# A two-block transformer layer on one core: every SBUF tile given whole 128-byte lines

## The chip, the core and the metric

The kernel runs on one core of one Trainium2 chip. The metric is the device time of one execution in microseconds (us), as the median of several runs. A core has a tensor engine (TensorE), which multiplies matrices into PSUM; a vector engine (VectorE) and a scalar engine (ScalarE), which work elementwise; GpSimd; and SyncE (SP), which here only issues DMAs. [...] The change concerns where in SBUF a tile begins.

## The reference, cut to what matters

Two blocks on 256 tokens of 1024 features, everything in float32. The first is modulated by a condition `c`:

```python
mod = silu(c) @ w_ada + b_ada                       # nine vectors of 1024
h = x + 0.5 * g1 * swiglu(modulate(rmsnorm(x)), w_ff1_gate, w_ff1_up, w_ff1_down)
h = h + g2 * token_mixing(modulate(rmsnorm(h)))     # gated linear attention and block attention
h = h + 0.5 * g3 * swiglu(modulate(rmsnorm(h)), w_ff2_gate, w_ff2_up, w_ff2_down)
x = rmsnorm(h)
x = x + hybrid_mixer(rmsnorm(x))                    # gated delta rule and mLSTM
x = x + memory_cross_attention(rmsnorm(x), rmsnorm(mem))
x = x + peer_ffn(rmsnorm(x))                        # 16384 experts, 8 heads, the 16 best of each
return rmsnorm(x)
```

`peer_ffn` scores every token against 2 × 128 keys per head, picks 16 experts per head, and sums gate × gelu(u_e · x) × v_e over them. The kernel forms the products with both whole tables (16384 × 1024 each) and uses the gates as a mask.

## The kernel before, in words

**Products.** Nearly all time goes into products of weights with 256 tokens. To keep float32 accuracy, each operand is split into a high and a low part of type float32r (hi = rounded copy, lo = rest), and three products are summed: hi·hi, hi·lo, lo·hi. A weight chunk of 128 x 1024 values (512 KB) is loaded by an SP DMA into a tile `raw` (L253), ScalarE casts it to `whi` (L254), VectorE subtracts to get `wlo` (L255). `raw` has three buffers and `whi`, `wlo` two, in each of two pools (`wa`, `wb`), taken in turn, so up to six chunks are loaded ahead. In the last part of the program, where only `wa` is left, a third pair of buffers, `wpair`, sits where `hT` was.

There are two forms of product. `linear_steps` has the weights stationary and the activations moving, 256 columns at a time (L305 to L307):

```python
mm(ps, wh, xh[:, kk, :], start=(kk == 0), stop=False)
mm(ps, wh, xl[:, kk, :], start=False, stop=False)
mm(ps, wl, xh[:, kk, :], start=False, stop=(kk == KT - 1))
```

`tm_steps` and `v_mm` have the activations stationary and the weights moving, 512 columns at a time. Every matmul has the line L192, that of the helper `mm(o, l, r)`, where `l` is the stationary operand and `r` the moving one. The profile names them as out<-moving,stationary: `mm<-uh,whi` has `uh` moving. `uh`, `ul` are the split activations (one pair of tiles for all norms), `hh`, `hl` the split hidden tile of an FFN (one pair in each), `mh`, `ml` the split memory, `oah` to `obl` and `xoh`, `xol` the split results of attentions, `wh`, `wl` a split column of expert weights. The products of attention and recurrences are plain float32 (`sm` tiles).

**Stages** in order of time (us of the profiled execution): modulation and first norm (0 to 38), FFN1 gate and up (38 to 172), FFN1 down and memory values (172 to 240), mixer 1 (240 to 435), FFN2 (435 to 636), memory keys and values, mixer 2 (to 860), cross attention (to 915), expert queries, first expert table with the choice of experts (to 1145) and with the gate matrices (to 1395), second expert table (to the end).

**Order of the work.** The program is written as generators that are woven together; a scheduler of the framework then orders each engine's instructions by priority and dependencies. A load into a tile has to wait for whoever last used that memory, so the place of a tile in SBUF also decides what its load waits for and when it is put into SP's queue.

**Tiles and their places.** A tile comes from a pool, `pool.tile(shape, dtype, name=..., tag=..., bufs=...)`; its size in a partition is rounded up to a multiple of 32 bytes, and tiles follow each other. Since `epsc` and `mean` have one column, `cols` 220 and so on, the large tiles behind them begin at any multiple of 32 bytes. The built program has these places, by the remainder of the byte address by 128:

| tiles | before | with the change |
|---|---|---|
| `uh`, `ul`, `hT`, `raw`, `whi`, `wlo`, `wpair` | 64 | 0 |
| `hh`, `hl` of FFN1 | 0 | 0 |
| `hh`, `hl` of FFN2 | 96 | 0 |
| `mh`, `ml`, `oah` to `obl`, `xoh`, `xol` | 96 | 0 |
| `wh`, `wl` | 64 | 0 |
| float32: `dm`, `m`, `dt`, `xs` | 0 | 0 |
| float32: `cvgq`, `cvgk` and the like | 64 | 0 |
| float32: `gv`, `at`, `gq`, `gk`, `xV`, `xpt` | 96 | 0 |

Slices that a product reads within a tile are whole multiples of 512 bytes, so they have their tile's remainder.

Of the kernel before, what the change touches and what calls it, by code (L numbers as in the profile page):

```python
# [33 lines left out]
# column pack: name -> number of columns  # L34
# [109 lines left out]
def _consts():  # L144
    """Arrays that depend on shapes alone."""
# [12 lines left out]
    # bucket of each distance; index x stands for distance 255 - x  # L158
# [15 lines left out]
    # selectors of packed rows: 0-3 row h; 4-7 rows h, 32+h, 64+h; 8-11 minus row 32+h  # L174
# [10 lines left out]
# ----------------------------------------------------------------- device code  # L185
def body(tc, A, out):
# [7 lines left out]
    cp = es.enter_context(tc.tile_pool(name="cp", bufs=1))  # L194
    wa = es.enter_context(tc.tile_pool(name="wa", bufs=2))
    pmm = es.enter_context(tc.tile_pool(name="pmm", bufs=4, space=PSUM))
    psm = es.enter_context(tc.tile_pool(name="psm", bufs=4, space=PSUM))
    dr = es.enter_context(tc.tile_pool(name="dr", bufs=1, space=DRAM))


    # ---- constants and small inputs
# [25 lines left out]
    # ---- weights: raw chunk -> exact pair (hi, lo), 12 bits each  # L227
    class Weights:
# [6 lines left out]
        def ahead(self, src, shape):  # L235
            """make the next chunk now, for a product further on"""
# [23 lines left out]
    def split(hi, lo, src):  # L260
        """src (SBUF or PSUM, fp32) -> hi, lo (float32r)"""
# [8 lines left out]
    def later(n=100000):  # L270
        """instructions that fill what the following ones leave idle"""
# [5 lines left out]
    def weave(main, side, n, m):  # L277
        """n steps of main, then m of side, in turn"""
# [9 lines left out]
    def linear_steps(w, KT, ms, xh, xl, evac):  # L288
        """feature-major output tiles [128, 256]; w [MT, 128, KT, 128]"""
# [26 lines left out]
    def tm_steps(w, n, xh, xl, evac):  # L316
        """token-major output [128 tokens, 512]; w [n, 4, 128, 2, 512]"""
# [17 lines left out]
    def sum_sq(pool, src, w=None):  # L335
        """mean over the 1024 features of (src * w)^2, a column per 128 tokens (PSUM)"""
# [11 lines left out]
    def rsqrt(pool, ms):  # L348
        """1 / sqrt(ms + eps), columns"""
        r = pool.tile([P, 2], F32, name="rr", tag="rr", bufs=4)  # L350
        act.activation(r, ms, AF.Sqrt, bias=epsc)  # L351
        r2 = pool.tile([P, 2], F32, name="rr2", tag="rr2", bufs=4)
# [3 lines left out]
    def spread(pool, r):  # L356
        """columns [tokens, 2] -> the row of 256 tokens on every partition (PSUM)"""
# [18 lines left out]
    def norm_apply(pool, src, r, hi, lo, a, b):  # L376
        """hi + lo = src * r * a + b"""
# [11 lines left out]
    # ================================================================ block 1  # L389
    wb_es = ExitStack()  # L390
    wb = wb_es.enter_context(tc.tile_pool(name="wb", bufs=2))
    W.pools.append(wb)
    npool = wb_es.enter_context(tc.tile_pool(name="npool", bufs=1))
    b1_es = ExitStack()
    kvp = b1_es.enter_context(tc.tile_pool(name="kvp", bufs=1))
# [5 lines left out]
    # silu(c) on every partition; mod = w_ada^T silu(c) + b_ada, feature-major  # L401
    kt_es = ExitStack()
    kt = kt_es.enter_context(tc.tile_pool(name="kvt", bufs=1))
# [8 lines left out]
    def ada_steps(js, cb=cb, bufs=None):  # L412
        """columns js of the modulation; bufs: memory for the weights"""
        o = _COFF["bada"][0]
        for j in js:
# [6 lines left out]
            if j // 8 in (1, 4, 7):  # L422
                # norm * (1 + scale)
# [13 lines left out]
    # K^T and V of the memory, kept in DRAM until the cross attention; made in pieces  # L437
    # where the tensor engine would wait for a norm
# [41 lines left out]
    # the modulation of the first norm, shift and scale in turn  # L480
# [14 lines left out]
    def ffn(name, i, fill, more):  # L495
        with tc.tile_pool(name=name, bufs=1) as fp:
# [43 lines left out]
    # ---------------------------------------------------------------- mixer 1  # L540
    with tc.tile_pool(name="mx", bufs=1) as mp:
        # bias[p, k] at distance 128 + p - k, kept at x = 127 - p + k
# [50 lines left out]
        # gate of the normalised GLA output: silu(gog) * norm  # L593
# [4 lines left out]
        # ---- GLA: log decay, cumulated within each 128 tokens  # L598
# [15 lines left out]
        # ---- attention matrices A^T[j, i], merged from levels of halved blocks;  # L614
        # heads of even and odd number sit in different halves of the partitions
# [37 lines left out]
        # between the two 128-token tiles  # L653
# [11 lines left out]
        # ---- outputs, norm per head, gate  # L665
# [4 lines left out]
        oa = [mp.tile([P, 4, P], F32, name="oa", tag="z", bufs=3) for _ in range(2)]  # L670
        for t in range(2):
# [6 lines left out]
            ss = mp.tile([P, 4], F32, name="gss", tag="gss", bufs=2)  # L678
# [9 lines left out]
        def to_fm(src, hi, lo, n):  # L688
            """token-major blocks src(t, h) [128, 128] -> hi, lo [128, n, 256]"""
# [8 lines left out]
        # ---- MoBA: one block of keys, so causal softmax attention  # L698
        def softmax_rows(pool, lg, n, tagp):
            """lg [128, n] -> normalised in place"""  # L700
            mx = pool.tile([P, 1], F32, name="smx", tag=tagp + "mx", bufs=3)
            dve.tensor_reduce(mx, lg, AX.X, OP.max, negate=True)
            sm = pool.tile([P, 1], F32, name="ssm", tag=tagp + "sm", bufs=3)
            act.activation(lg, lg, AF.Exp, bias=mx, accum_out=sm)
            rc = pool.tile([P, 1], F32, name="src", tag=tagp + "rc", bufs=3)
# [23 lines left out]
        # ---- merge; the gates are (1 + tanh(x/2)) / 2, their half is taken at the end  # L729
        g5 = mp.tile([P, 8], F32, name="g5")  # L730
        dve.tensor_scalar(g5, mod[:, 40:48], 0.5, None, OP.mult)
# [20 lines left out]
    # two norms in a row: x = h r1 g, and the mean square of x is r1^2 mean (h g)^2  # L752
# [16 lines left out]
    # ================================================================ block 2  # L769
    with tc.tile_pool(name="hx", bufs=1) as hp:  # L770
# [25 lines left out]
        def conv(ps, name, j, dst):  # L796
            """depthwise causal convolution over the tokens (half of it), then silu(x) =
            (1 + tanh(x/2)) x/2"""
# [51 lines left out]
        # ---- gates: rows 0-3 g_a, 32-35 g_b, 64-67 m_i, 96-99 m_f  # L850
# [534 lines left out]
```

## Time and profile before

| | |
|---|---|
| median of 3 runs | 1763.02 us (1762.89 to 1763.87) |
| profiled execution, its span | 1756.4 us |
| TensorE busy | 1700.8 us, 97% |
| VectorE busy | 1253.9 us, 71% |
| ScalarE busy | 1025.0 us, 58% |
| DMA, mean | 191 GB/s, 336.32 MB |

The profiled execution is known by its span, from its first to its last instruction; the times of the runs are taken around the execution and are some 6.6 us longer. Busy times of TensorE come from modelled ends of pipelined matmuls: a matmul's 0.28 us is the time from its start to its result, and several overlap. What a matmul costs in a row of them is the distance between their starts. TensorE's granted clock is nearly always that of full speed.

### The profile page before, as it was taken

Reading aid. Unit: us, or ns where it says so; the run is one execution under the profiler, and the core shown is the slowest. Engines: PE = TensorE matmul, PEld = TensorE weight load, DVE = VectorE, ACT = ScalarE, POOL = GpSimd, SP = SyncE. Lnnn points to the kernel's source line nnn. Section 1 sums busy time; section 2 is a strip of 40 time slices with the busy share of each in tenths; the row PEclk is TensorE's granted clock in tenths of the full one; section 3 lists DMA queues with packets and bytes.
Section 4 is the critical chain, followed back from the end, with each engine's and each line's share of the span. In section 5 each row is a group of like instructions: output and inputs, shape, how many; then the busy total and the mean of one; then the engine's idle time right before and its main releaser. Section 6 shows DMA issues by size and latency. Waiting matters only on the chain.

```text
span 1756.4 us, 31700 instructions
## 1 busy us (share of the span) xinstructions
PE 1700.8 (97%) x12298; PEld 1603.0 (91%) x12298; DVE 1253.9 (71%) x2223; ACT 1025.0 (58%) x1977; POOL 4.0 (0%) x36
## 2 busy tenths in 40 slices
PE   3999999899999999999989999999999999999998
PEld 2999998899999999888889999999999988888886
DVE  7888677767855569866566689488999755555555
ACT  5556466565644458666654445588877544444544
POOL 0000000000000000000000000000000000000000
PEclk9999999999999999999999999999999999999999
DMA  9888788345855657216325555544444555555554
GB/s 345 326 294 314 222 283 319 121 144 181 287 192 175 186 181 246 91 37 220 131 79 196 177 174 179 192 144 136 142 142 136 192 190 194 192 180 192 192 193 143
DMA packets 97716, 336.32 MB, mean 191 GB/s; under 512 B 10988, under 2 KB 16541, under 8 KB 96926
## 3 DMA queue, kind: packets, MB, share of 16 engines
q1 hardware_dynamic: 94828, 330.63, 55.8%
q10 hardware_dynamic: 2738, 3.68, 0.6%
q8 instruction: 96, 1.57, 0.4%
q14 instruction: 54, 0.44, 0.1%
HBM read 329.02 MB, written 5.25 MB: 190 GB/s over the span
## 4 chain that ended last, share of the span: by engine, by line
PE 90%; DVE 4%; ACT 3%; DMA 2%; issue 2%; SPq 0%; DVEq 0%; ACTq 0%
PE mm L192 81%; PE sm L192 8%; DMA wr<-in_w_ada 1%; DVE wlo L255 1%; DMA mT<-in_memT 0%; ACT whi L254 0%; DVE wr L419 0%; DVE at L651 0%; DVE ac L806 0%; DVE sqa L342 0%; PE sm L693 0%; PE sm L1117 0%; DVE xn L487 0%; PE sm L720 0%; ACT L351 0%
## 5 line engine op out<-in xcount | busy, mean ns | idle before, releaser
L255 DVE TENSOR_TENSOR wlo<-raw,whi 128x1024 fp32r<-128x1024 f32 (+1 forms) x448 | 542.6, 1213 | 255.0 <-ACT whi L254 253.9
L254 ACT CAST whi<-raw 128x1024 fp32r<-128x1024 f32 (+1 forms) x448 | 465.7, 1041 | 402.0 <-PE mm L192 285.6
L192 PE MATMUL mm<-uh,whi 128*128 128x256 f32 x2064 | 592.2, 289 | 9.8 <-ACT whi L254 7.4
L192 PE MATMUL mm<-ul,whi 128*128 128x256 f32 x2064 | 587.7, 286 | 2.5 <-DVE ul L263 2.0
L192 PE MATMUL mm<-uh,wlo 128*128 128x256 f32 x2064 | 586.8, 285 | 0.7 <-DVE wlo L255 0.7
L192 PEld LDWEIGHTS mm<-uh,whi 128*128 128x128 f32 x2064 | 397.4, 193 | 12.0 <-ACT whi L254 8.2
L192 PEld LDWEIGHTS mm<-ul,whi 128*128 128x128 f32 x2064 | 398.0, 193 | 3.7 <-DVE ul L263 2.2
L192 PEld LDWEIGHTS mm<-uh,wlo 128*128 128x128 f32 x2064 | 397.8, 193 | 1.9 <-DVE wlo L255 1.3
L255 DVE TENSOR_TENSOR wpair<-raw,wpair 128x1024 fp32r<-128x1024 f32 x90 | 110.0, 1222 | 82.4 <-ACT wpair L254 82.4
L192 PE MATMUL mm<-uh,wpair 128*128 128x256 f32 x768 | 148.1, 286 | 0.0
L192 PE MATMUL mm<-whi,wh 128*128 128x512 f32 x344 | 133.8, 390 | 1.7 <-ACT wh L262 1.7
L192 PE MATMUL mm<-whi,wl 128*128 128x512 f32 x344 | 134.8, 392 | 0.1
L192 PE MATMUL mm<-wlo,wh 128*128 128x512 f32 x344 | 134.6, 391 | 0.0
L254 ACT CAST wpair<-raw 128x1024 fp32r<-128x1024 f32 x90 | 94.6, 1051 | 65.2 <-PE mm L192 65.2
L192 PEld LDWEIGHTS mm<-uh,wpair 128*128 128x128 f32 x768 | 122.9, 191 | 0.0
L192 PE MATMUL mm<-wpair,wh 128*128 128x512 f32 x336 | 110.2, 389 | 0.0
L192 PE MATMUL mm<-ul,wpair 128*128 128x256 f32 x384 | 108.6, 283 | 0.0
L419 DVE SCALAR_TENSOR_TENSOR wr<-wr,cb 128x1024 f32<-128x1024 f32 x72 | 87.4, 1220 | 19.7 <-DMA wr<-in_w_ada 19.5
L192 PE MATMUL mm<-hh,whi 128*128 128x256 f32 x352 | 98.7, 280 | 0.0
L192 PE MATMUL mm<-hl,whi 128*128 128x256 f32 x352 | 98.6, 280 | 0.0
L192 PE MATMUL mm<-hh,wlo 128*128 128x256 f32 x352 | 98.6, 280 | 0.0
L192 PEld LDWEIGHTS mm<-whi,wh 128*128 128x128 f32 x344 | 64.7, 188 | 15.3 <-ACT wh L262 1.9
(838 smaller groups left out, 2621.9 us busy)
## 6 DMA issues: line engine op xcount, KB each, us to landing
raw<-in_pu SPq DMA_DIRECT2D x128, 512.0 KB, 3.2
raw<-in_pv SPq DMA_DIRECT2D x128, 512.0 KB, 3.2
raw<-in_ff_gu SPq DMA_DIRECT2D x88, 512.0 KB, 4.3
wr<-in_w_ada SPq DMA_DIRECT2D x72, 512.0 KB, 5.9
raw<-in_in_fm SPq DMA_DIRECT2D x34, 512.0 KB, 4.3
raw<-in_ff_dn SPq DMA_DIRECT2D x32, 512.0 KB, 4.1
raw<-in_in_tm SPq DMA_DIRECT2D x24, 512.0 KB, 5.6
raw<-in_in_gab SPq DMA_DIRECT2D x16, 512.0 KB, 4.3
```

The source lines that it names most:

```text
L192: pe.matmul(o, l, r, start=start, stop=stop)
L254: act.copy(hi[:, :n], raw[:, :n])
L255: dve.tensor_tensor(lo[:, :n], raw[:, :n], hi[:, :n].bitcast(F32), OP.subtract)
L419: dve.scalar_tensor_tensor(wr, wr, 1.0, cb, OP.mult, OP.mult, accum_out=mod[:, j:j + 1])
```

## The change

Each pool is wrapped: `Pools` hands out pools, and for those in SBUF a `Lines` object, which makes every tile's size in a partition a multiple of `LINE` = 128 bytes by adding columns at its end, and returns the part that was asked for. To save places, small columns are joined: `rr` and `rr2` of `rsqrt` are two halves of a tile of four columns; the three columns of `softmax_rows` (`smx`, `ssm`, `src`) one tile `sm3`; the two `gss` tiles one; `warm` and the two `fss` tiles one. `g5`, half of eight columns of `mod`, is no tile of its own any more: the scaling is done in `mod` in place. Two tags of `s2` become one. Comments were dropped, so line numbers differ by 35 and more.

```diff
+LINE = 128
+class Pools:
+    def __init__(self, tc):
+        self.tc = tc
+    @contextmanager
+    def __call__(self, **kw):
+        with self.tc.tile_pool(**kw) as pool:
+            yield pool if "space" in kw else Lines(pool)
+class Lines:
+    def __init__(self, pool):
+        self.pool = pool
+    def tile(self, shape, dtype, **kw):
+        n = int(np.prod(shape[1:]))
+        per = LINE // 4
+        if n % per == 0:
+            return self.pool.tile(shape, dtype, **kw)
+        kw.setdefault("tag", kw["name"])
+        t = self.pool.tile([shape[0], -(-n // per) * per], dtype, **kw)[:, :n]
+        if len(shape) == 2:
+            return t
+        d = "abc"[:len(shape) - 1]
+        return t.rearrange(f"p ({' '.join(d)}) -> p {' '.join(d)}", **dict(zip(d, shape[1:])))
...
-    cp = es.enter_context(tc.tile_pool(name="cp", bufs=1))
-    wa = es.enter_context(tc.tile_pool(name="wa", bufs=2))
+    tile_pool = Pools(tc)
+    cp = es.enter_context(tile_pool(name="cp", bufs=1))
+    wa = es.enter_context(tile_pool(name="wa", bufs=2))
...
-        r = pool.tile([P, 2], F32, name="rr", tag="rr", bufs=4)
+        rr = pool.tile([P, 4], F32, name="rr", tag="rr", bufs=4)
+        r, r2 = rr[:, 0:2], rr[:, 2:4]
         act.activation(r, ms, AF.Sqrt, bias=epsc)
-        r2 = pool.tile([P, 2], F32, name="rr2", tag="rr2", bufs=4)
         dve.reciprocal(r2, r)
...
+        gss = mp.tile([P, 2, 4], F32, name="gss")
...
-            ss = mp.tile([P, 4], F32, name="gss", tag="gss", bufs=2)
+            ss = gss[:, t, :]
...
-            mx = pool.tile([P, 1], F32, name="smx", tag=tagp + "mx", bufs=3)
+            c3 = pool.tile([P, 4], F32, name="sm3", tag=tagp + "m3", bufs=3)
+            mx, sm, rc = c3[:, 0:1], c3[:, 1:2], c3[:, 2:3]
...
-        g5 = mp.tile([P, 8], F32, name="g5")
-        dve.tensor_scalar(g5, mod[:, 40:48], 0.5, None, OP.mult)
+        g5 = mod[:, 40:48]
+        dve.tensor_scalar(g5, g5, 0.5, None, OP.mult)
...
+        fss = vp.tile([P, 5], F32, name="fss")
...
-                act.activation(vp.tile([P, 1], F32, name="warm"), epsc, AF.Sqrt)
+                act.activation(fss[:, 4:5], epsc, AF.Sqrt)
...
-            ss = vp.tile([P, 2], F32, name="fss", tag="fss", bufs=2)
+            ss = fss[:, 2 * t:2 * t + 2]
```

All other tiles are written as before; their places move with those in front of them. The counts of instructions of every engine are the same. Their order differs in two places.

SP's queue at the start of FFN2, before (`raw` are weight chunks, `wr` blocks of `w_ada`, `cb` a copy of silu(c)):

```order
L253 DMA raw<-in_w_out 128x1024 x8
L253 DMA raw<-in_xa_k 128x1024 x4
L253 DMA raw<-in_ff_gu 128x1024 x5
L431 DMA cb_5332<-cd 128x1024
L418 DMA wr_5334<-in_w_ada 128x1024
L253 DMA raw<-in_ff_gu 128x1024
L418 DMA wr_5335<-in_w_ada 128x1024
L253 DMA raw<-in_ff_gu 128x1024
L418 DMA wr_5334<-in_w_ada 128x1024
L253 DMA raw<-in_ff_gu 128x1024
```

and with the change:

```order
L288 DMA raw<-in_w_out 128x1024 x8
L288 DMA raw<-in_xa_k 128x1024 x2
L466 DMA cb_5310<-cd 128x1024
L288 DMA raw<-in_xa_k 128x1024 x2
L453 DMA wr_5312<-in_w_ada 128x1024
L288 DMA raw<-in_ff_gu 128x1024
L453 DMA wr_5313<-in_w_ada 128x1024
L288 DMA raw<-in_ff_gu 128x1024
L453 DMA wr_5312<-in_w_ada 128x1024
L288 DMA raw<-in_ff_gu 128x1024
```

The copy `cb` went ahead of two chunks of `xa_k`, and the first blocks of `w_ada` ahead of the chunks of `ff_gu` that had been five in a row. The tiles moved with all others; `cb` lies over the tiles `zb`, `zl` and `oa` of the GLA stage in both, and its load now also waits for TensorE, which read `oa`.

VectorE's queue at the end of FFN1's down product and in the norm of mixer 1, before (`g` is g5, `sqa` the sum of squares of the norm):

```order
L255 TENSOR_TENSOR wlo<-raw,whi 128x1024
L342 TENSOR_TENSOR sqa<-sqa,sq 128x256
L255 TENSOR_TENSOR wlo<-raw,whi 128x1024 x2
L533 SCALAR_TENSOR_TENSOR hT<-mm,half,hT 128x256
L731 TENSOR_SCALAR g_3965<-mod 128x8
L255 TENSOR_TENSOR wlo<-raw,whi 128x1024
L342 TENSOR_TENSOR sqa<-sqa,sq 128x256
L255 TENSOR_TENSOR wlo<-raw,whi 128x1024
```

and with the change, where the scaling now stands with the first columns of that product:

```order
L568 SCALAR_TENSOR_TENSOR hT<-mm,half,hT 128x256
L454 SCALAR_TENSOR_TENSOR wr,mod<-wr,cb 128x1024
L290 TENSOR_TENSOR wlo<-raw,whi 128x1024
L377 TENSOR_TENSOR sqa<-sqa,sq 128x256
L766 TENSOR_SCALAR mod<-mod 128x8
L290 TENSOR_TENSOR wlo<-raw,whi 128x1024
L290 TENSOR_TENSOR wlo<-raw,whi 128x768
L568 SCALAR_TENSOR_TENSOR hT<-mm,half,hT 128x256
```

The scaling, now in `mod` itself, stands some thirty rows earlier; the rows around it are the same.

## Rows read from the trace of the kernel before

**Rows 1.** The page: the span; its section 1, busy time, share of the span and count of instructions of each engine (PE is TensorE, PEld its weight loads, DVE VectorE, ACT ScalarE); the second line of its section 4, the chain of work that ended last, by line.

```profile
span 1756.4 us, 31700 instructions
...
PE 1700.8 (97%) x12298; PEld 1603.0 (91%) x12298; DVE 1253.9 (71%) x2223; ACT 1025.0 (58%) x1977; POOL 4.0 (0%) x36
...
PE mm L192 81%; PE sm L192 8%; DMA wr<-in_w_ada 1%; DVE wlo L255 1%; DMA mT<-in_memT 0%; ACT whi L254 0%; DVE wr L419 0%; DVE at L651 0%; DVE ac L806 0%; DVE sqa L342 0%; PE sm L693 0%; PE sm L1117 0%; DVE xn L487 0%; PE sm L720 0%; ACT L351 0%
```

**Rows 2.** The table of stretches, four of them: start and end in us, length, then for PE, PEld, DVE, ACT and POOL the busy us and the number of instructions, the granted TensorE clock as a share of full speed, the mean busy share of the DMA engines, GB/s moved.

```profile
38.00:172.00 134.00, 133.62 (x1083) 131.94 (x1084) 111.19 (x169) 80.89 (x153) 0.00 (x0) 0.99 0.88 318
440.00:570.00 130.00, 130.00 (x1085) 129.85 (x1084) 85.13 (x121) 69.60 (x115) 0.00 (x0) 1.00 0.67 219
1037.00:1145.00 108.00, 108.00 (x904) 108.00 (x903) 83.34 (x259) 61.56 (x99) 0.00 (x0) 1.00 0.55 181
1145.00:1395.00 250.00, 249.19 (x2116) 248.98 (x2114) 229.93 (x323) 192.00 (x513) 0.00 (x0) 1.00 0.42 141
```

**Rows 3.** The timeline of TensorE in FFN2's up product, two instructions that are eight steps apart, each a matmul of its own in between: start us, us, engine, line, operation, result<-moving operand,stationary operand, array part used, shape of the moving operand.

```profile
499.94 0.28 PE L192 MATMUL mm<-uh,whi 128*128 128x256 f32 x1
...
500.90 0.28 PE L192 MATMUL mm<-uh,wlo 128*128 128x256 f32 x1
```

**Rows 4.** The same in the last stage (experts, second table), two instructions that are twenty steps apart.

```profile
1500.05 0.39 PE L192 MATMUL mm<-whi,wh 128*128 128x512 f32 x1
...
1504.58 0.39 PE L192 MATMUL mm<-wlo,wh 128*128 128x512 f32 x1
```

**Rows 5.** The same in FFN1's down product, nine steps apart.

```profile
199.94 0.28 PE L192 MATMUL mm<-hh,whi 128*128 128x256 f32 x1
...
200.96 0.28 PE L192 MATMUL mm<-hh,whi 128*128 128x256 f32 x1
```

**Rows 6.** The same in FFN2's down product, nine steps apart.

```profile
599.90 0.28 PE L192 MATMUL mm<-hl,whi 128*128 128x256 f32 x1
...
600.96 0.28 PE L192 MATMUL mm<-hl,whi 128*128 128x256 f32 x1
```

**Rows 7.** The same in the product for the values of the memory, six steps apart.

```profile
652.53 0.39 PE L192 MATMUL mm<-whi,ml 128*128 128x512 f32 x1
...
653.93 0.39 PE L192 MATMUL mm<-whi,ml 128*128 128x512 f32 x1
```

**Rows 8.** The timeline of TensorE at three places with plain float32 products, where equal instructions in a row are one line: start of the first, us to the end of the last, operation, operands, shape, count.

```profile
345.83 0.83 PE L192 MATMUL sm<-gv,at 128*128 128x128 f32 x6
...
721.12 0.83 PE L192 MATMUL sm<-cvgq,cvgk 128*128 128x128 f32 x6
...
727.43 0.72 PE L192 MATMUL sm<-dm,m 128*128 128x128 f32 x5
```

**Rows 9.** The groups of TensorE's matmuls with different shapes kept apart: line, operation, operands, shape, count | busy us, mean ns of one (a latency) | idle time before them and what ended it.

```profile
L192 PE MATMUL mm<-uh,whi 128*128 128x256 f32 x2064 | 592.2, 289 | 9.8 <-ACT whi L254 7.4 <-ACT uh L372 1.4 <-ACT uh L262 1.0
...
L192 PE MATMUL mm<-uh,wpair 128*128 128x256 f32 x768 | 148.1, 286 | 0.0
...
L192 PE MATMUL mm<-whi,wh 128*128 128x512 f32 x344 | 133.8, 390 | 1.7 <-ACT wh L262 1.7
L192 PE MATMUL mm<-wpair,wh 128*128 128x512 f32 x336 | 110.2, 389 | 0.0
L192 PE MATMUL mm<-ul,wpair 128*128 128x256 f32 x384 | 108.6, 283 | 0.0
L192 PE MATMUL mm<-hh,whi 128*128 128x256 f32 x352 | 98.7, 280 | 0.0
...
L192 PE MATMUL mm<-wpair,wl 128*128 128x512 f32 x168 | 65.4, 389 | 0.0
L192 PE MATMUL mm<-whi,uh 128*128 128x512 f32 x96 | 37.8, 394 | 0.1
...
L192 PE MATMUL mm<-xoh,whi 128*128 128x256 f32 x64 | 18.0, 287 | 0.0
L192 PE MATMUL mm<-mh,whi 128*128 128x256 f32 x64 | 17.9, 280 | 0.0
...
L192 PE MATMUL mm<-whi,mh 128*128 128x512 f32 x32 | 12.9, 405 | 0.0
...
L192 PE MATMUL mm<-oah,whi 128*128 128x256 f32 x32 | 9.1, 286 | 0.0
```

**Rows 10.** The chain of waits in order of time, three pieces of it: start us, us, what, number of instructions.

```profile
37.99 99.82 PE mm L192 x817
...
152.34 7.47 DMA wr<-in_w_ada
...
1397.19 352.10 PE mm L192 x1561
```

**Rows 11.** The groups of VectorE by line, first from 100 to 172 us (FFN1), then from 470 to 570 us (FFN2): the low half of the FFN's hidden tile.

```profile
L263 DVE TENSOR_TENSOR hl<-sy,hh 128x256 fp32r<-128x256 f32 x12 | 5.0, 419 | 0.0
...
L263 DVE TENSOR_TENSOR hl<-sy,hh 128x256 fp32r<-128x256 f32 x18 | 7.5, 418 | 0.0
```

**Rows 12.** The timeline of the SP queue at the start of FFN2: start us, us, line, what it loads, count.

```profile
421.93 11.80 SPq L253 DMA_DIRECT2D raw<-in_ff_gu  x5
434.59 0.33 SPq L431 DMA_DIRECT2D cb<-cd  x1
434.96 0.42 SPq L418 DMA_DIRECT2D wr<-in_w_ada  x1
```

More of the change, by code (lines that the diff above doesn't have):

```diff
@@ L192, in mm @@
         pe.matmul(o, l, r, start=start, stop=stop)
-    cp = es.enter_context(tc.tile_pool(name="cp", bufs=1))
-    wa = es.enter_context(tc.tile_pool(name="wa", bufs=2))
-    pmm = es.enter_context(tc.tile_pool(name="pmm", bufs=4, space=PSUM))
-    psm = es.enter_context(tc.tile_pool(name="psm", bufs=4, space=PSUM))
-    dr = es.enter_context(tc.tile_pool(name="dr", bufs=1, space=DRAM))
+    tile_pool = Pools(tc)
+    cp = es.enter_context(tile_pool(name="cp", bufs=1))
+    wa = es.enter_context(tile_pool(name="wa", bufs=2))
+    pmm = es.enter_context(tile_pool(name="pmm", bufs=4, space=PSUM))
+    psm = es.enter_context(tile_pool(name="psm", bufs=4, space=PSUM))
+    dr = es.enter_context(tile_pool(name="dr", bufs=1, space=DRAM))
     cols = cp.tile([P, NCOL], F32, name="cols")
@@ L390, in body @@
     wb_es = ExitStack()
-    wb = wb_es.enter_context(tc.tile_pool(name="wb", bufs=2))
+    wb = wb_es.enter_context(tile_pool(name="wb", bufs=2))
     W.pools.append(wb)
-    npool = wb_es.enter_context(tc.tile_pool(name="npool", bufs=1))
+    npool = wb_es.enter_context(tile_pool(name="npool", bufs=1))
     b1_es = ExitStack()
-    kvp = b1_es.enter_context(tc.tile_pool(name="kvp", bufs=1))
+    kvp = b1_es.enter_context(tile_pool(name="kvp", bufs=1))
     mod = kvp.tile([P, NMOD * KD], F32, name="mod")
@@ L402, in body @@
     kt_es = ExitStack()
-    kt = kt_es.enter_context(tc.tile_pool(name="kvt", bufs=1))
+    kt = kt_es.enter_context(tile_pool(name="kvt", bufs=1))
     cb = kt.tile([P, D], F32, name="cb")
@@ L495, in ffn @@
     def ffn(name, i, fill, more):
-        with tc.tile_pool(name=name, bufs=1) as fp:
+        with tile_pool(name=name, bufs=1) as fp:
             uh, ul = new_u()
@@ L538, in body @@
     kt_es.close()
-    with tc.tile_pool(name="mx", bufs=1) as mp:
+    with tile_pool(name="mx", bufs=1) as mp:
         bias = mp.tile([P, 4, T], F32, name="tbias")
@@ L699, in softmax_rows @@
         def softmax_rows(pool, lg, n, tagp):
-            mx = pool.tile([P, 1], F32, name="smx", tag=tagp + "mx", bufs=3)
+            c3 = pool.tile([P, 4], F32, name="sm3", tag=tagp + "m3", bufs=3)
+            mx, sm, rc = c3[:, 0:1], c3[:, 1:2], c3[:, 2:3]
             dve.tensor_reduce(mx, lg, AX.X, OP.max, negate=True)
-            sm = pool.tile([P, 1], F32, name="ssm", tag=tagp + "sm", bufs=3)
             act.activation(lg, lg, AF.Exp, bias=mx, accum_out=sm)
-            rc = pool.tile([P, 1], F32, name="src", tag=tagp + "rc", bufs=3)
             dve.reciprocal(rc, sm)
@@ L767, in body @@
     b1_es.close()
-    with tc.tile_pool(name="hx", bufs=1) as hp:
+    with tile_pool(name="hx", bufs=1) as hp:
         lvm = hp.tile([P, 7, P], I32, name="lvm2")
@@ L1090, in body @@
                lambda m, ps: dve.tensor_tensor(hT[:, m, :], ps, hT[:, m, :], OP.add))
-    with tc.tile_pool(name="xa", bufs=1) as xp_:
+    with tile_pool(name="xa", bufs=1) as xp_:
         xK = xp_.tile([P, KD, T], F32, name="xK")
@@ L1145, in body @@
     ap_es = ExitStack()
-    app = ap_es.enter_context(tc.tile_pool(name="app", bufs=1))
+    app = ap_es.enter_context(tile_pool(name="app", bufs=1))
     NU1, NU2 = 24, 60
@@ L1170, in u_ev @@
             dve.tensor_tensor(aw[:, j, :g], aw[:, j, :g], z[:, :g], OP.mult)
-    with tc.tile_pool(name="sel", bufs=1) as sp_:
+    with tile_pool(name="sel", bufs=1) as sp_:
         tv = [sp_.tile([P, 16, 16], F32, name=f"tv{t}") for t in range(2)]
@@ L1176, in top16 @@
         def top16(s, v, ix, n):
-            s2 = sp_.tile([P, n], F32, name="s2", tag=f"s2{n}", bufs=2)
+            s2 = sp_.tile([P, n], F32, name="s2", tag="s2", bufs=2)
             dve.max(v[:, 0:8], s)
@@ L1293, in body @@
         weave(u_steps(NU1, NU2, u_ev), picks(), 1, 1)
-    with tc.tile_pool(name="gp", bufs=1) as gpp:
+    with tile_pool(name="gp", bufs=1) as gpp:
         done["pool"] = gpp
@@ L1319, in body @@
         weave(u_steps(NU2, NEXP, u_ev), gates(), 1, 1)
-    with tc.tile_pool(name="vp", bufs=1) as vp:
+    with tile_pool(name="vp", bufs=1) as vp:
         h3 = cp.tile([P, KD, T], F32, name="h3", tag="uh")
```

## The prediction

> **What bounds the kernel now.** Read the page's busy times and its chain of waits first: TensorE is busy for 97% of the span, and 81% of the chain that ended last lies on the line L192, the products that accumulate in the "mm" tiles [rows 1]. So a time per product counts nearly in full. The stage table says the same by place: between 440 and 570 us and between 1037 and 1145 us TensorE never stops, while VectorE has a quarter to a third of the time free and the DMA engines a third or more [rows 2]. Two stages have little to spare beside TensorE: 38 to 172 us, where the DMA share is 0.88, and 1145 to 1395 us, where VectorE is busy for 229.93 of 250 us. [...]
>
> The durations in the trace are latencies (0.28 us) and not what a product costs; that is the distance from one start to the next. I read it in the timeline for five pairs of places in a 128-byte line (stationary operand first, then moving):
> - 64 and 64, 256 columns: 0.96 us for 8 steps, **120.0 ns** [rows 3].
> - 64 and 64, 512 columns: 4.53 us for 20 steps, **226.5 ns** [rows 4].
> - 64 and 0, 256 columns (FFN1's down product): 1.02 us for 9 steps, **113.3 ns** [rows 5].
> - 64 and 96, 256 columns (FFN2's down product): 1.06 us for 9 steps, **117.8 ns** [rows 6].
> - 96 and 64, 512 columns (values of the memory): 1.40 us for 6 steps, **233.3 ns** [rows 7].
>
> The first two differ by 256 columns and 106.5 ns, that is 2.4 columns per ns; what is left is the same 13.3 ns per product whatever its length. In the other three this fixed part is 6.6, 11.1 and 20 ns. FFN1 and FFN2 run the same loop on the same shapes, only with `hh` and `hl` at another place, and differ by 4.5 ns: where the operands start in a line has a price, and the change sets all of them to 0.
>
> **The change, step by step.** No instruction is added or dropped. The pair 0 and 0 occurs nowhere in the trace with float32r products, so its fixed part has to be bounded. Above: 20 ns, the dearest placement seen. Below: 0, since 106.7 ns for 256 columns is the rate itself. The nearest rows are the plain float32 products: with moving operands at 96, 64 and 0, five steps take 0.83 − 0.28 us (the latency of the last one), five again, and four take 0.72 − 0.28 us, 0.11 us each whatever the place [rows 8]. That is the time of 256 columns at the rate above and about 3 ns. I take **3 ns**, because it is the same engine with no trace of placement in it, and because the cheapest float32r case (6.6 ns) still has its weights at 64.
>
> [...]
>
> Counts are from the groups by shape [rows 9]. 256 columns at 64 and 64: `uh,whi` 2064, as many `ul,whi` and `uh,wlo`, and with `wpair` 768 + 384, together 7344. 512 columns at 64 and 64: three times 344, then 336 + 168, and three times 96, together 1824. `hh` and `hl`: three times 352, half at 0 (528) and half at 96. At 96 also `mh` and `xoh`, three times 64 each, and `oah` and `obh`, six times 32: 528 + 576 = 1104. Stationary at 96: three times 32 = 96. Then
> - 9168 × (13.3 − 3) = 94.4 us
> - 528 × (6.6 − 3) = 1.9 us
> - 1104 × (11.1 − 3) = 8.9 us
> - 96 × (20 − 3) = 1.6 us
>
> Together 106.9 us. All these products take 881 + 414 + 60 + 130 + 22 = 1507 us at the present distances, and 81% of 1756.4, 1423 us, of them are on the chain: a factor of 0.944, **100.9 us**.
>
> What is late next takes some back. From 38 to 172 us, 1083 products would give 11 us, but the DMA engines have 12% left, and the chain there ends in a wait for a `w_ada` block [rows 10]: I take 5 us off. From 1145 to 1395 us three quarters of 2116 products would give 16 us; VectorE would then be busy for 230 of 234 us: 4 us off. The last 352 us are products almost without a gap [rows 10], and give in full. Sum: 100.9 − 9 = **92 us**.
>
> Edits with no price of their own: VectorE's operation does not see the place (`hl` takes 419 ns with `hh` at 0 and 418 at 96 [rows 11]), nor does a joined column cost an instruction. The scaling of `mod` on VectorE goes earlier, 128x8 elements in a stretch where TensorE has queued products ahead. On SP's queue the copy `cb` and the `w_ada` blocks of FFN2 move ahead of five weight chunks and two of `xa_k`. If `cb` could still go no sooner than 434.59 us, chunks would start up to 434.59 − 421.93 = 12.7 us late [rows 12]; six chunks in buffers, 24 products of 120 ns each, cover 17 us. I take 0 (0 to +5 us in the range): its new waiting partner is a tile of the GLA stage, read long before.
>
> The profiled span is 1756.4 us and the median of the runs 1763.02, 6.6 us more around it, which the change does not touch. Forecast: 1763 − 92 = **1671 us**.
>
> **Rivals.** *Only one operand's place counts.* The fixed part of 0 and 0 is then that of FFN1's down product, 6.6 ns. For it: no row has a stationary operand at 0. Against it: a stationary operand at 96 rather than 64 costs 6.7 ns more with the moving one unchanged [rows 4, 7]. Sum: 9168 × 6.7 + 1104 × 4.5 + 96 × 13.4 ns = 67.7 us, times 0.944, less 4 us of new limits: 60 us, 1703 us.
>
> *The distance between the two operands counts, not the line* (slower). Both read the same memory while a product runs; if starts at equal places clash, 0 and 0 clash like 64 and 64. Then 13.3 ns stay where they were, and the cheap placements are lost: 528 × 6.7 + 1104 × 2.2 − 96 × 6.7 ns = 5.3 us, on the chain **+5 us: 1768 us**. It decides from a fixed part of 12.8 ns up (where gains and losses cancel); at 20 ns it would be 10,896 × 7.2 × 0.944, +74 us. For it: in the trace the equal pair is dearer than 64 with 0 and 64 with 96. Against it: 96 with 64 is dearer still.
>
> *Nothing changes.* A line shorter than 128 bytes, 32 or 16, makes all present places whole already, and the 6.7 ns of FFN1 would come from something else that differs there. Time: 1763 us. Against it: the distance is 113.3 ns in every step of that stretch and 117.8 in the same loop later. [...]
>
> **Chances.** Both operands at 3 ns or near: 0.52. One operand: 0.27. Distance: 0.10. Nothing: 0.10. Stages more bound by DMA than thought, so that the gain is under 45 us: 0.01. The range takes the first two. Its low end is the fixed part 0: 139.6 × 0.944 = 132 us, 14 off for the limits, 1645 us; its high end is the second case without its cover, 1703 and 5 for the queue and 5 for DMA, 1713 us. A measurement of this kernel tells 0.2%, 3.5 us, from no change. Faster by more: 0.79; within: 0.10; slower: 0.11 (the distance case, and a little of the rest).
>
> **What would show it.** In the new timeline the starts of `uh,whi` should be 109 to 110 ns apart and those of `whi,wh` 216; 113 and 220 mean the second case, 120 and 227 one of the last two, and FFN1's down product tells these apart (113 against 120). Plain float32 groups must stay at 0.11 us. From 1145 to 1395 us VectorE should come to 97% or more. I am wrong if the products keep their distances, or if they shorten and the chain moves to DMA waits.

## The result, and the profile after

The changed kernel is **slower**: 1773.22 us, median of six runs (1770.98 to 1776.68), against 1762.91 us for six runs of the kernel before (1753.68 to 1763.87); ratio 1.0077, 95% interval 1.0055 to 1.0100, that is 10 to 18 us or under 1% more (the medians themselves lie 10.3 us apart). 1671 was forecast; the nearest case in the prediction is the second rival, distance, at 1768.

The page of the kernel after (span, busy times, chain by line) answers to [rows 1]:

```profile
span 1773.7 us, 31704 instructions
...
PE 1714.6 (97%) x12298; PEld 1608.2 (91%) x12298; DVE 1254.3 (71%) x2223; ACT 1025.4 (58%) x1977; POOL 4.0 (0%) x36
...
PE mm L226 80%; PE sm L226 8%; DMA wr<-in_w_ada 2%; DVE wlo L290 1%; ACT whi L289 1%; DVE wr L454 1%; DVE at L686 0%; DVE ac L841 0%; DVE sqa L377 0%; DVE ul L298 0%; DMA raw<-in_ff_gu 0%; PE sm L1152 0%; DVE xn L522 0%; PE sm L755 0%; PE sm L729 0%
```

TensorE still bounds the kernel, with the same shares; it is busy for 14 us longer, and VectorE as long as before, to 0.4 us. So the products themselves are the first suspects. The timeline of TensorE in the kernel after, in the stages of [rows 3 to 7], two instructions of each, 60 steps apart in the first three pairs, then 15 and 58:

```profile
199.82 0.28 PE L226 MATMUL mm<-hh,whi 128*128 128x256 f32 x1
...
207.03 0.28 PE L226 MATMUL mm<-hh,whi 128*128 128x256 f32 x1
...
499.95 0.28 PE L226 MATMUL mm<-uh,whi 128*128 128x256 f32 x1
...
507.15 0.28 PE L226 MATMUL mm<-uh,whi 128*128 128x256 f32 x1
...
599.80 0.28 PE L226 MATMUL mm<-hh,whi 128*128 128x256 f32 x1
...
606.92 0.28 PE L226 MATMUL mm<-hh,whi 128*128 128x256 f32 x1
...
656.12 0.39 PE L226 MATMUL mm<-wlo,mh 128*128 128x512 f32 x1
...
659.60 0.39 PE L226 MATMUL mm<-wlo,mh 128*128 128x512 f32 x1
...
1499.98 0.40 PE L226 MATMUL mm<-whi,wh 128*128 128x512 f32 x1
...
1513.47 0.40 PE L226 MATMUL mm<-wpair,wl 128*128 128x512 f32 x1
```

- FFN1's down product: 7.21 us for 60 steps, **120 ns**; it was 113.3 [rows 5].
- FFN2's up product: 7.20 us, **120.0 ns**, unchanged [rows 3].
- FFN2's down product: 7.12 us, **118.7 ns**; over all its steps it was 117.3 before (117.8 over the nine of [rows 6]).
- Values of the memory: 3.48 us for 15 steps, 232.0 ns; it was 233.3 [rows 7].
- Second table of the experts: 13.49 us for 58 steps, **232.6 ns**; it was 226.5 [rows 4]. Over all its steps it is 232.4, and it was 226.7.

No product came near 110 ns. Two groups became dearer, and they carry the loss: 528 × 6.7 = 3.5 us in FFN1, and with 512 columns 1536 × 5.7 = 8.8 us in the last stage; 1104 products at 1.3 ns more add 1.4 us. Together 13.7 us, within the interval of the result. The table of stretches, first of the kernel before, then of the kernel after, each from the first down product of FFN1 to the memory values, and the last stage:

```profile
164.20:229.90 65.70, 65.32 (x543) 63.65 (x543) 45.58 (x69) 33.33 (x52) 0.41 (x2) 0.97 0.74 233
1395.90:1756.40 360.50, 353.96 (x1568) 292.94 (x1568) 200.46 (x262) 175.03 (x264) 0.00 (x0) 0.99 0.56 189
...
164.00:234.70 70.70, 70.14 (x542) 67.68 (x542) 45.83 (x70) 33.38 (x52) 0.41 (x2) 0.95 0.68 218
1404.60:1773.60 369.00, 362.55 (x1568) 293.91 (x1568) 200.34 (x262) 174.60 (x264) 0.00 (x0) 0.99 0.55 184
```

The first became 5.0 us longer, the second 8.5. (Of the 5.0 us, 3.5 are the products; the granted clock was 0.95 instead of 0.97 there.)

What the two dearer groups have in common is not seen in the remainder by 128 that the table of places gave. In the remainder by 256 of the address in SBUF, the memory on the chip in which the tiles lie, it is: `hh` of FFN1 was 64 bytes below `whi` and is now at the same remainder; `wh` and `wl` were at the same remainder as `whi` and are now 128 bytes off. (Below, a distance is the start of the moving operand less that of the stationary one, modulo 256: FFN1's down product went from 192 to 0, the second table from 0 to 128, and the products with `uh`, `ul` moving stayed at 0.)

### The profile page after: what moved, and what is told of

It is laid out like the page before. It is cut to its first block, busy times and chain, and to the rows that moved or that the text cites. A ratio compares the mean times of both kernels' runs of the same rounds, so it can differ in the third digit from the quotient of the medians.

```text
span 1773.7 us, 31704 instructions
## 1 busy us (share of the span) xinstructions
PE 1714.6 (97%) x12298; PEld 1608.2 (91%) x12298; DVE 1254.3 (71%) x2223; ACT 1025.4 (58%) x1977; POOL 4.0 (0%) x36
## 4 chain that ended last, share of the span: by engine, by line
PE 88%; DVE 5%; ACT 3%; DMA 2%; issue 1%; SPq 0%; DVEq 0%; ACTq 0%
PE mm L226 80%; PE sm L226 8%; DMA wr<-in_w_ada 2%; DVE wlo L290 1%; ACT whi L289 1%; DVE wr L454 1%; DVE at L686 0%; DVE ac L841 0%; DVE sqa L377 0%; DVE ul L298 0%; DMA raw<-in_ff_gu 0%; PE sm L1152 0%; DVE xn L522 0%; PE sm L755 0%; PE sm L729 0%
```

## The experiments

Theory **distance**: what a float32r product costs depends on the start of its moving operand less the start of its stationary one, modulo 256 bytes; lines as such do nothing. Rival **places**: each operand's own place has a price. Rival **surroundings**: the traffic of other engines made the differences. Rival **order**: the loss comes from the loads that moved at FFN2, or from the clock.

### e1_sweep: products alone

```python
# stationary from byte s of one tile, moving from byte m of another, three matmuls per k
group("sa", 0, 0, 256);  group("sb", 0, 32, 256)    # ... s: distances 0, 32, ..., 224
group("ta", 64, 64, 256)                            # t: the same, both 64 bytes later
group("wa", 0, 0, 512)                              # w: 512 columns
```

> Products alone: no block of the transformer is computed, only 38 groups of 48 float32r matmuls (24 for plain float32) with operands cut out of two tiles at chosen bytes; the output is not the reference's. Groups s: stationary at 0 (mod 128), moving 0, 32, ... 224 bytes further (mod 256), 256 columns; groups t: the same distances with both 64 bytes later; groups w: 512 columns; x: finer steps, the stationary operand moved instead, whole steps of 256 and 512; f: plain float32. Theory distance (the start of the moving operand less that of the stationary one, modulo 256 bytes, sets the cost): s and t agree within 0.5 ns at every distance; 0 gives 120.0 ns, 192 gives 113.3, 160 and 32 about 117, 128 about 118.7; 512 columns give 226.7 at 0, 233 at 96, 232 at 128; steps of 256 and 512 give 120 again, f the same four times. Rival places (each operand's own place in a line or in 256 bytes has its price): t differs from s by several ns at most distances, since both operands moved by half a line. Rival surroundings (the differences came from other work that reads SBUF at the same time): all groups of 256 columns alike, near 109 or near 120 ns.

The timeline of TensorE of this run, a line for each group: start, us to the end of the last, operands, count. The pace is (us − 0.28)/47 for 256 columns, (us − 0.39)/47 else:

```profile
23.63 5.92 PE L223 MATMUL sa<-mv,st 128*128 128x256 f32 x48
29.39 5.82 PE L223 MATMUL sb<-mv,st 128*128 128x256 f32 x48
35.05 5.82 PE L223 MATMUL sc<-mv,st 128*128 128x256 f32 x48
40.71 5.91 PE L223 MATMUL sd<-mv,st 128*128 128x256 f32 x48
46.45 5.86 PE L223 MATMUL se<-mv,st 128*128 128x256 f32 x48
52.15 5.86 PE L223 MATMUL sf<-mv,st 128*128 128x256 f32 x48
57.84 5.82 PE L223 MATMUL sg<-mv,st 128*128 128x256 f32 x48
63.50 5.84 PE L223 MATMUL sh<-mv,st 128*128 128x256 f32 x48
69.17 5.91 PE L223 MATMUL ta<-mv,st 128*128 128x256 f32 x48
74.92 5.82 PE L223 MATMUL tb<-mv,st 128*128 128x256 f32 x48
...
86.24 5.91 PE L223 MATMUL td<-mv,st 128*128 128x256 f32 x48
...
103.38 5.82 PE L223 MATMUL tg<-mv,st 128*128 128x256 f32 x48
...
114.71 11.06 PE L223 MATMUL wa<-mv,st 128*128 128x512 f32 x48
...
136.81 11.16 PE L223 MATMUL wc<-mv,st 128*128 128x512 f32 x48
...
181.46 11.35 PE L223 MATMUL wg<-mv,st 128*128 128x512 f32 x48
...
243.66 5.92 PE L223 MATMUL xh<-mv,st 128*128 128x256 f32 x48
...
255.18 10.53 PE L223 MATMUL fa<-mf,sf 128*128 128x256 f32 x48
...
286.26 10.52 PE L223 MATMUL fd<-mf,sf 128*128 128x256 f32 x48
```

At 256 columns: 120.0 ns at distance 0 (sa), 117.9 at 32 and 64 (sb, sc), 119.8 at 96 (sd), 118.7 at 128 and 160, 117.9 at 192 (sg), 118.3 at 224. The groups t agree with s within 0.3 ns, and a step of 256 bytes (xh) costs what 0 costs: **distance, not place, and not surroundings**, since no other engine worked here but ScalarE, which copied eight columns behind each group. This holds for groups in which all products have one distance, as those of the kernel do; e8 mixes two. At 512 columns the order is another: distance 0 is the cheapest (227.0), 64 gives 229.1, 192 gives 233.2. Plain float32 did not show it here (fa, fd: 215.7 ns). Three expectations failed. 192 gave 117.9 and not the 113.3 of FFN1, which e4 takes up. 160 gave 118.7 and not about 117, though FFN2's down product in the kernel before, at that distance, keeps 117.3 over all its steps. 512 columns at 128 gave 233.4 and not 232, though the second table of the changed kernel keeps 232.4. These last two, 1.4 and 1.0 ns, stay open: distance orders the paces, but does not fix each to a nanosecond.

### e2_uh_first: only uh and ul move in the kernel before

```diff
     gp.memset(ones, 1.0)
+    first_u = (cp.tile([P, KD, T], F32R, name="uh", tag="uh"),
+               cp.tile([P, KD, T], F32R, name="ul", tag="ul"))
     mean = cp.tile([P, 1], F32, name="mean")
...
-            uh, ul = new_u()
+            uh, ul = first_u if i == 0 else new_u()
```

> The kernel before with one edit: the tiles uh and ul are made ahead of mean and epsc, so that uh and ul begin at 0 (mod 256) while whi, wlo, wpair stay at 64; every other product keeps its places. Theory distance: the 7344 products with uh or ul moving go from 120.0 to the 113.3 ns of FFN1's down product, which has the same distance (192); 7344 x 6.7 ns = 49 us, 46 on the chain, 4 or 5 lost to DMA and VectorE: about 1721 us. The 288 products with uh stationary get distance 64, not yet seen: between 6 us less and 3 us more. Rival surroundings: the products stay at 120 ns, 1763 us. Rival places: uh at 0 and whi at 64 are the places of FFN1's down product, so 113.3 as well; this run does not tell it from the first theory, the sweep does.

1739.25 us (four runs), ratio 0.9893, interval 0.9872 to 0.9914: 21 us less, half of what was expected. The timeline of TensorE, two pairs of instructions that are 60 steps apart, first in FFN1, then in FFN2:

```profile
90.02 0.28 PE L192 MATMUL mm<-uh,whi 128*128 128x256 f32 x1
...
97.08 0.28 PE L192 MATMUL mm<-uh,whi 128*128 128x256 f32 x1
...
499.87 0.28 PE L192 MATMUL mm<-uh,whi 128*128 128x256 f32 x1
...
506.67 0.28 PE L192 MATMUL mm<-uh,whi 128*128 128x256 f32 x1
```

7.06 us, **117.7 ns**, in FFN1 and 6.80 us, **113.3 ns**, in FFN2, with the same tiles and the same distance. Each pace holds from the start of a stretch to its end (some 1000 products); over all products with `uh` or `ul` moving the mean is 115.5. So at this distance the pace has two states. The gain in products is 7344 × 4.4 = 32 us, 30 on the chain; 9 of them are lost, and the page's chain by line now has VectorE's `wlo` with 3% and `aw` with 2%, where [rows 1] have 1% and nothing. That fits the limit that the prediction saw in the stage with the gate matrices; how much of the 9 us it took was not measured.

### e3_dist_back: the changed kernel with two old distances

```diff
+            if i == 0:
+                gp.memset(fp.pool.tile([P, 48], F32, name="pad"), 0.0)
             hh = fp.tile([P, KF, T], F32R, name="hh")
...
-        fss = vp.tile([P, 5], F32, name="fss")          # ahead of wh, wl
...
             if j == NEXP // 2:
+                fss = vp.tile([P, 5], F32, name="fss")  # behind them
```

> The kernel with whole lines, and two sets of tiles moved so that their distances are again those of the kernel before: wh and wl by 128 bytes less (fss is made after them), and hh, hl of FFN1 by 192 bytes more (a tile of 192 bytes ahead of them, set to zero by GpSimd). The order of instructions stays. Theory distance: FFN1's down product goes back from 120.0 to 113.3 ns (528 x 6.7 ns = 3.5 us) and the second table of the experts from 232.3 to 226.7 ns (1536 x 5.6 ns = 8.6 us), together 12 us: 1761 us, within 4 us of the kernel before. Rival order (the loss comes from the loads that moved at the start of FFN2, or from the clock): stays near 1773 us with the stage of the second table as long as in the changed kernel, or it shortens and the total does not.

1760.71 us (ten runs), ratio 1.0007, interval 0.9990 to 1.0023: **the loss is gone**, with whole lines everywhere but in `hh`, `hl` of FFN1 and what lies behind them there, and with the order of instructions of the changed kernel. The table of stretches of this run, the same two pieces of the program:

```profile
165.00:230.90 65.90, 65.26 (x542) 63.59 (x543) 45.72 (x70) 33.36 (x52) 0.41 (x2) 0.97 0.71 231
1397.20:1757.60 360.40, 353.90 (x1568) 292.92 (x1568) 200.41 (x262) 175.02 (x264) 0.00 (x0) 0.99 0.56 188
```

65.90 and 360.40 us, as in the kernel before, against 70.70 and 369.00. The rival order falls: every engine runs its instructions in the order of the changed kernel, and the joined columns, the scaling in place and the moved loads together cost at most the 4 us that the interval leaves.

### e4_modes: bursts after a short break

```python
for n in range(1, 9):
    for _ in range(n):        # plain float32, 128 columns
        pe.matmul(z[:, :P], sf[:, 0:P], mf[:, 0:P], start=True, stop=True)
    group(name, 0, 32 * i, 256, reps=1)
```

> Products alone again (no block of the transformer is computed): for each of the eight distances (da 0, db 32, ... dh 224 bytes, 256 columns) eight bursts of 24 float32r matmuls, the first after one plain float32 matmul of 128 columns, the next after two, and so on to eight; then the same at 512 columns for the distances 0, 64 and 192, six bursts each. In the kernel with uh moved, the same products ran at 113.4 ns in some bursts and at 117.8 in others. Theory phase (at a distance other than 0 the pace has more than one state, and where the burst starts decides which; the state then holds for the whole burst): bursts of one distance fall into two or more values, dg (192) into 113.4 and 117.8, chosen by the number of plain products before; da stays at 120.0 in all. Rival neighbours (traffic of other engines on SBUF makes the difference): every burst of one distance has the same pace here, 117.8 for dg, since no other engine works.

The timeline of TensorE, one burst at distance 0 (da), one at 32 (db), then the first four of eight at 192 (dg), after one to four plain products:

```profile
23.51 3.12 PE L223 MATMUL da<-mv,st 128*128 128x256 f32 x24
...
54.55 3.05 PE L223 MATMUL db<-mv,st 128*128 128x256 f32 x24
...
208.51 2.98 PE L223 MATMUL dg<-mv,st 128*128 128x256 f32 x24
...
211.70 3.07 PE L223 MATMUL dg<-mv,st 128*128 128x256 f32 x24
...
215.20 3.07 PE L223 MATMUL dg<-mv,st 128*128 128x256 f32 x24
...
218.92 2.98 PE L223 MATMUL dg<-mv,st 128*128 128x256 f32 x24
```

At 192 a burst takes 2.98 or 3.07 us; the first step is 0.20 us after a break, and the steps behind it settle at **113.3** or **117.8 ns**: fast after one, four, five and eight plain products, slow after two, three, six and seven. (The bursts pf of e8, also at 192, repeat this in another program for one to six.) At 0 all eight take 120, at 32 all take 116.5 to 116.9 (in the sweep, behind another group without a break, 117.9), at 128 they take 118.5 and 120.0 in turn. The bursts of 512 columns show it at distance 0, with 228.7 and 227.1 in turn; 64 gives 229.3 and 192 gives 233.3. The theory of phase holds, with no other engine at work but for ScalarE's copies: **what comes just before a stream picks its state, and the stream keeps it.** In the traces of e2, e5 and e9, 81 of 82 unbroken streams of 30 or more products with `uh` or `ul` moving stay in one state, the longest for 1014 products. Whether it is the moment of the start or the count of plain products that picks was not tried apart.

### e5, e6, e7: whole lines, three distances for uh and ul

```diff
+    gp.memset(cp.pool.tile([P, 16], F32, name="pad0"), 0.0)     # 8 for e6, 24 for e7
+    first_u = (cp.tile([P, KD, T], F32R, name="uh", tag="uh"),
+               cp.tile([P, KD, T], F32R, name="ul", tag="ul"))
+    gp.memset(cp.pool.tile([P, 16], F32, name="pad1"), 0.0)     # 24 and 8
```

(On top of e3; `mean` and `epsc` share one tile, ahead of `pad0` in e5 and behind `pad1` in the others; `hT` and `whi` stay at 0 modulo 256.)

> The kernel with whole lines and the two sets of tiles of the last such run (wh and wl 128 bytes less, hh and hl of FFN1 192 bytes more), and now uh and ul too: they come ahead of hT, 64 bytes before a line's end (192 modulo 256), while hT, whi, wlo and wpair stay at the start of a line of 256 bytes. Theory distance with phase: 7344 products at distance 192, half of the bursts at 113.4 and half at 117.8 ns, on average 4.4 ns less than 120: 32 us, 30 on the chain, some 9 lost to DMA, VectorE and the products with uh stationary (229 instead of 226.7 ns): 21 us less than 1760.7, about 1740 us, the same as the kernel before with uh moved. Rival places (it matters whether whi is at the start of a line): clearly other than 1739, by more than 5 us.

> As the run at distance 192, but uh and ul at 32 modulo 256. From the sweeps the products take 116.7 to 117.9 ns at this distance whatever the burst: 7344 x 2.1 to 3.3 ns = 15 to 24 us, and 288 products with uh stationary at distance 224 cost 6.4 ns more each, 2 us; with some 3 us lost to VectorE and DMA: 1744 to 1752 us. Rival: only the distance 192 is good in the kernel, and this one stays at 1760 us.

> As the run at distance 192, but uh and ul at 96 modulo 256. From the sweeps 119.8 ns at this distance: 7344 x 0.2 ns = 1.5 us less, and 288 products with uh stationary at distance 160 cost 7.4 ns more each, 2 us: 1761 us, no change against the kernel before. Rival: any distance but 0 helps, and it comes to 1740 to 1750 us.

| distance | median us (runs) | ratio, interval | expected us | mean step with uh, ul moving |
|---|---|---|---|---|
| 192 (e5) | 1747.42 (6) | 0.9921, 0.9902 to 0.9940 | 1740 | 115.7 ns |
| 32 (e6) | 1746.36 (4) | 0.9934, 0.9915 to 0.9953 | 1744 to 1752 | 117.0 ns |
| 96 (e7) | 1763.95 (10) | 1.0023, 1.0012 to 1.0034 | 1761 | 119.9 ns |

The distances order the kernels as the sweep said. e7 is slower than the kernel before by 2 to 6 us, a little more than expected; 2.0 us of it are the 288 products with `uh` or `ul` stationary, at 234.2 instead of 227.2 ns. e5 came out 8 us above e2, which was the condition set for the rival places. The distances between products speak against that rival: 115.7 against 115.5 ns in e2. The rest is told by where the shorter steps fell. In e5 it was FFN1's up product that ran at 113.4 and FFN2's at 117.8, in e2 the other way round. The chain of waits of e5 in FFN1:

```profile
37.54 62.22 PE mm L226 x531
...
99.82 6.44 DMA wr<-in_w_ada
...
109.06 6.65 DMA wr<-in_w_ada
...
120.64 5.68 DMA wr<-in_w_ada
```

With faster products FFN1 waits three times for a `w_ada` block, 5.7 to 6.7 us each, which the chain of the kernel before does not show there [rows 10]. In this run the blocks came too late for shorter steps to give anything: the last step of FFN1's up product starts 4.9 us earlier than in e2 (156.70 against 161.63 us), but that of its down product 0.7 us later (226.03 against 225.35). In FFN2, where nothing else is late, e5 had the longer ones: 1015 products × 4.4 = 4.5 us. FFN2's down product at 120.0 instead of 117.3 ns adds 1.4 us. Together that would be 6 to 7 of the 8 us; it was not tried apart.

### e8_pairs: which stationary operand does a moving one meet?

```python
for i in range(24):                       # two pairs of places in turn
    l, r = (a, b)[i % 2]                  # bytes of stationary, of moving
```

> Products alone (no block of the transformer is computed): bursts of 24 float32r matmuls of 256 columns, each with its own weight load, in turn with two pairs of places; six bursts of each, after one to six plain float32 matmuls. It asks which stationary operand a moving one meets: its own, or that of the next matmul, whose load runs while this one streams. Bytes of (stationary, moving) in turn: pa (0,0) and (0,0); pb (0,0) and (64,64): own distance 0, distance to the next load 192 and 64; pc (0,64) and (64,0): own distance 64 and 192, to the next load 0; pd (0,0) and (128,128): own 0, next 128; pe (0,128) and (128,0): own 128, next 0; pf (0,192) twice: both 192. Theory next load: pc and pe take 120.0 ns like pa, pb about 115.6 to 117.8 and pd about 118.6 to 120. Rival own load: pb and pd take 120.0 like pa, pc 117.8 or less. Both alike if the products' own and next loads overlap with it in equal parts: all between.

The timeline of TensorE, bursts of pa, pb, pc (two of them), pd and pe:

```profile
23.25 3.12 PE L237 MATMUL pa<-mv,st 128*128 128x256 f32 x24
...
48.45 3.05 PE L237 MATMUL pb<-mv,st 128*128 128x256 f32 x24
...
66.73 3.05 PE L237 MATMUL pc<-mv,st 128*128 128x256 f32 x24
...
73.52 3.13 PE L237 MATMUL pc<-mv,st 128*128 128x256 f32 x24
...
88.58 3.05 PE L237 MATMUL pd<-mv,st 128*128 128x256 f32 x24
...
110.18 3.05 PE L237 MATMUL pe<-mv,st 128*128 128x256 f32 x24
```

pa holds 120 ns (3.12 us). pb and pd, whose own distance is 0, take 116.5 to 118.0, so that the own distance alone does not make 120. pc, whose distance to the next load is 0, takes 116.7 after one plain product and 119.1 to 120.2 else; pe, whose distance to the next load is 0 as well, takes 117.0 in all six bursts, so that this distance alone does not make 120 either. pf, with 192 for both, takes the two paces of e4. (In the kernel before, at 499.82 us, the load for the next product starts with the product that runs, takes 0.19 us, and the next product follows 0.12 us after that start.) Neither form of the theory fits: 120 in every burst came only where both distances are 0. The rule of the sweep is thus one for streams with a single distance, and which load meets which read **stays open**.

### e9_best: nearly all products of 256 columns at 192

```diff
-    mod = kvp.tile([P, NMOD * KD], F32, name="mod")
+    mod = kvp.tile([P, NMOD * KD + 8], F32, name="mod")[:, :NMOD * KD]
...
+            if i == 0:
+                gp.memset(fp.tile([P, 56], F32, name="pad"), 0.0)
             hh = fp.tile([P, KF, T], F32R, name="hh")
...
+        gp.memset(xp_.tile([P, 40], F32, name="pad"), 0.0)
         xoh = xp_.tile([P, KD, T], F32R, name="xoh")
```

> The kernel before with uh and ul moved as in the second run (distance 192), and hh, hl of FFN2, mh, ml, oah to obl, xoh, xol moved to 0 modulo 256 as well, so that nearly all products of 256 columns have the distance 192; wh, wl stay at distance 0 for 512 columns, mh and ml as stationary operands get 64 instead of 96. Theory distance: 1104 products from 117.3 to between 113.4 and 117.8, 0 to 4 us, and 96 from 233.4 to 229: about 2 us less than 1739, 1734 to 1740 us. Rival: the second run was all there is to gain, and this one is within 1 us of it; they differ by less than two runs of one kernel do, so that the trace's distances have to tell it: hh of FFN2 at 117.3 or below.

(The eight columns more in `mod` move what lies behind it by 32 bytes; the pad of 224 bytes brings `hh` of FFN1 back to 0 modulo 256.)

1741.73 us (six runs, 1733.66 to 1745.26), ratio 0.9897, interval 0.9872 to 0.9922; 1734 to 1740 was expected. The timeline of TensorE in FFN2's down product, 60 steps apart:

```profile
580.17 0.28 PE L192 MATMUL mm<-hh,wlo 128*128 128x256 f32 x1
...
586.97 0.28 PE L192 MATMUL mm<-hh,wlo 128*128 128x256 f32 x1
```

6.80 us, 113.3 ns, and not 117.3: the move does to the product what it should. The median is not below e2's, and the intervals overlap. Streams that pick their state anew in each run could make the spread of 12 us, but with one trace of each kernel that is not shown. Both beat the kernel before by 18 to 21 us; between them nothing is decided.

## Why the prediction was wrong, point by point

- **What bounds the kernel** was right: the distance between the starts of products sets the time, in both directions (e2, 21 us less, and the kernel after, 10.3 us more).
- **The five paces were right, their reading was not.** The step that failed is "where the operands start in a line has a price, and the change sets all of them to 0". The pairs 64 with 64 and 64 with 0 were read as two places; they are two distances, 0 and 192. The change left the 7344 dear products at distance 0 and at 120.0 ns, so the term 9168 × (13.3 − 3) = 94.4 us held 75.6 us that did not come. With the distances set back and the tiles still on whole lines, the loss went (e3); with only `uh`, `ul` off distance 0, time was gained (e2, e5, e6).
- **The floor of 3 ns** was taken from plain float32, which showed no distance in e1 (215.7 ns at fa and fd). No float32r pair measured here, at any distance, took less than 113.3 ns: above the 106.7 ns that the prediction estimated for 256 columns from [rows 3, 4], a fixed part of 6.6 ns is the best, and 13.3 the dear end.
- **The terms of FFN1 and of the placed tiles** had the wrong sign: −1.9 us forecast for FFN1, +3.5 measured; −8.9 us for the 1104, +1.4 measured; the 96 memory products gained 0.1 instead of 1.6 us.
- **The terms of 512 columns** fell most. 1536 of the 1824 products, in the second table, were to gain 10.3 ns each and lost 5.7, 8.8 us in all, because `wh` and `wl` went from distance 0 to 128. At 512 columns distance 0 is the best of the eight measured, 227.0 ns against 233.4 at 128 (e1).
- **The rival distance** named the mechanism, at a chance of 0.10, and gave 1768. It missed the 8.8 us of the second table, since places were taken modulo 128, where nothing moves between `wh` and `whi`; with these it would have said 1777. That 1768 lies so near the 1773 measured is in part luck. What was held against it, 96 with 64 being the dearest, was a product of 512 columns, which follows its own order.
- **Edits priced at nothing** (joined columns, scaling in place, moved loads, VectorE) cost at most 4 us together: e3 has them all.
- **The limits** of DMA and VectorE showed where products did get faster (e2, e5), but were priced too low: the 9 us set against a gain of 101 went already with a gain of 30 on the chain (e2).
- **The 6.6 us** between the profiled span and the median, read as time around the execution, are not that: every run with its span on record takes 1.7 to 3.0 us more than that span, so that the profiled execution was a shorter one than the median. The forecast does not use them.
- **The rival of no change** fell too: places that are all multiples of 32 bytes gave 117.9 to 120.0 ns in e1, and FFN1's down product went from 113.3 to 120.0 ns with the change.
- How much of a pace is the weight load's is not shown: in the kernel before and after each of the 12298 matmul records has a load of its own ([rows 1] and the page of the kernel after), and no run took the load away.

## What to carry to other kernels

In these runs a stream of float32r matmuls that each load their weights had a pace that depended on how the two operands lie to each other (113.3 to 120.0 ns at 256 columns), so read the distance between starts in the timeline, not the duration (0.28 us at every one of these paces), for each pair of tiles, and take addresses modulo 256, not modulo a line (in e1 a step of 256 bytes cost what 0 costs, 120.0 ns, and one of 128 bytes 118.7). Rounding tiles up to 128-byte lines leaves only the distances 0 and 128. For 256 columns both are at the dear end (118.5 to 120.0 ns); for 512 columns 0 is the best (227.0 ns in e1) and 128 is not (233.4). Moving one pair of tiles to a better distance gained 21 us (e2), where aligning everything lost 10 to 18. Before a forecast from two paces, ask whether place or difference explains them: a third pair with both moved together decides it, in one short run of products alone.

## What the runs showed of the hardware that was not expected

- At distance 192 a stream of 256-column products runs at 113.4 or at 117.8 ns, the state is chosen when it starts and then holds for up to 1014 products, and breaks of one to eight plain products choose it in the pattern fast, slow, slow, fast (e4, and e8 again). What in the start decides is open.
- The best distance depends on the length: for 256 columns 0 is at the dear end (120.0; the others 113.3 to 120.0), for 512 it is the best (226.7 to 228.8, against 229 to 234).
- Runs of one kernel lie up to 12 us apart (e9), and up to 10 us in the kernel before; a forecast to 0.2% could not have been tested with three of them. In the kernel before the granted clock goes with it: of the 41 runs behind the experiments, those from 1764 us up have 0.990 or 0.991 and those under 1757 us 0.994 or 0.995. In e9 it does not: 0.990 in the shortest run, 0.993 in the longest.
